# Attention scores: two 64-row matmuls on two halves of the array in place of two 128-row ones

## The chip, the cores and the metric

The kernel runs on one core of a Trainium2 chip. The metric is device microseconds from the start to the end of one execution; three runs of the kernel before were timed, and one execution was profiled with all its instructions.

The engines are named as in the profile: PE is TensorE's matmul, PEld its weight load, DVE is VectorE, ACT ScalarE, POOL GpSimd, SP the engine whose queue issues the DMAs. A matmul in this program is always two instructions: a weight load of the stationary operand (LDWEIGHTS, on PEld) and the product with the moving operand (MATMUL, on PE). The array has 128 rows, over which a product contracts, and 128 columns.

## What is computed

The reference is one layer of a hybrid backbone: a gated linear attention and a differential attention run on the same normalised input, are gated, merged and projected. The change lies in the differential attention alone:

```
def diff_attention(q1, q2, k1, k2, v, lam):
    ...
        s1 = jnp.einsum('bhqd,bhkd->bhqk', qb1, k1).astype(jnp.float32) * scale
        s2 = jnp.einsum('bhqd,bhkd->bhqk', qb2, k2).astype(jnp.float32) * scale
        a = jax.nn.softmax(s1, axis=-1) - lam * jax.nn.softmax(s2, axis=-1)
        return jnp.einsum('bhqk,bhkv->bhqv', a.astype(v.dtype), v)
```

There are 8 heads, 1024 latent queries, and 1280 keys (256 of the context, then 1024 latent ones). Each head has two components, with queries and keys of their own (q1, k1 and q2, k2, 64 numbers each) and one value matrix of 128 columns. Everything is float32.

## The kernel before

**High and low parts.** PE multiplies numbers rounded to a shorter form (fp32r) in one pass. The kernel keeps accuracy by splitting a float32 operand into a rounded part, "high", and the rest, "low", and by adding up several products. For the scores the four products high by high, high by low, low by high and low by low fit into two matmuls, because a component has only 64 numbers and the array has 128 rows. A key tile holds the high parts of a component's keys in rows 0 to 63 and the low parts in rows 64 to 127, over all 1280 keys. A query tile holds the high queries (`Q[comp][:, 0]`) and the low queries (`Q[comp][:, 1]`), each written twice, in rows 0 to 63 and again in rows 64 to 127. The matmul with index j = 0 therefore gives high queries by (high + low keys), the one with j = 1 low queries by (high + low keys), and PSUM adds them up.

**A unit of the scores.** `att_scores` (line 1940) runs over 8 heads and 8 query tiles of 128 queries: 64 units. A unit's scores take five PSUM banks of 512 columns: two for the main part of component 0 (keys 0 to 1023), one shared by the tails of both components (keys 1024 to 1279 of component 0, keys 0 to 255 of component 1), and two for the main part of component 1 (keys 256 to 1279). In the tables at lines 2035 and 2036 each pair is the first key and the number of keys:

```
    TAIL = ((1024, 256), (0, 256))
    MAIN = (((0, 512), (512, 512)), ((256, 512), (768, 512)))
```

The helper `score` (line 1952) issues the two matmuls, j = 0 and j = 1, of one stretch of keys. So the main part of a component is four matmuls with 512 moving columns: bank 0 with j = 0 and 1, then bank 1 with j = 0 and 1. The tails add four matmuls with 256 columns. After the main part, VectorE takes the maximum over both banks (`att_max`, line 1991), and ScalarE makes the exponentials with their sum (`att_exp`, line 1998); VectorE joins the two components (`att_mix`), PE transposes the result (`att_tr`), its parts are split into high and low, and PE multiplies them with the values (`att_av`).

**What sets the order.** The program is written out once, by a planner (class `Driver`, line 59). Tasks are generators; a task that is due issues its instructions, and the planner keeps a clock of PE (`now`) and of the other engines with a cost for each instruction, so that each engine's instructions stand in an order fixed before the run. `mm` (line 348) issues a matmul and charges PE, for fp32r, 0.009 us plus 0.000428 us for each moving column, 0.228 us for 512 columns. A `yield AtPE(0)` lets other due tasks go in between. The order of the parts of the attention (scores "S", transposes "T", values "A") is a list made by `att_order` (line 1915). Gaps in PE's plan are filled with other projections' matmuls (`fill`, line 2194; in the profile "mb<-h,wt").

`banked` (line 359) tells the framework which PSUM bank an instruction of the scores touches, so that only instructions of other engines on the same bank are waited for.

**Loading keys and queries.** `att_keys` (line 1848) loads a head's keys: for each component one DMA of 64 rows by 1280 high parts and one of the low parts, from scratch in DRAM into one of three key buffers (the tile "hk" in the profile). The buffers are given back after the head's last query tile. `att_queries` (line 1873) loads the queries of two query tiles at a time, each part twice. All these DMAs are issued from SP's queue.

Of the kernel before, what the change touches and what calls it, by code (L numbers as in the profile page):

```python
# [20 lines left out]
P = 128  # L21
# [3 lines left out]
T = S + CTX  # L25
# [207 lines left out]
class Hybrid:  # L233
# [20 lines left out]
        mm=("psA", 3), tp=("psA", 2), edge=("sbE", 1), gs=("psA1", 1), go=("psA1", 1), gt=("psA1", 1),  # L254
# [90 lines left out]
            yield  # L345
        self.d.spawn(later(), AtPE(at), prio=-9)

    def mm(self, out, lhsT, rhs, start, stop, more=False):
        self.ins = self.nc.tensor.matmul(out, lhsT, rhs, start=start, stop=stop, skip_group_check=more).ins  # L349
        n = rhs.free_size()  # L350
        c = 0.009 + max(n, 230) * 0.000428 if rhs.dtype == F32R else 0.006 + max(4 * n, 470) / 2400
        return self.d.op("PE", c, [out], [lhsT, rhs])

    def mm3(self, out, sh, sl, mh, ml, first, last, more=False):
        self.mm(out, sh, mh, first, False, more)
# [1492 lines left out]
    def att_keys(self):  # L1848

        for hd in range(8):  # L1850
            c, x = hd // 4, hd % 4
            for i in range(10):
                yield self.ev_st["dk", c, i]
            if hd:
                yield self.ev_q[0, 1]
            else:
                yield self.gla_free[3]
                yield from self.acq("hc", 16)
                Driver.places = (T, 2 * T, 3 * T)
                self.hk = self.t("hk", [P, HK], F32R)  # L1860
            K = []
            for comp in range(2):
                rows = slice(64 * comp, 64 * comp + 64)
                yield from self.acq("kk")
                m = (2 * hd + comp) % 3
                kt = self.hk[:, m * T:(m + 1) * T]
                self.dma(kt[0:64], self.d_kT[0][c][x, rows])
                self.dma(kt[64:128], self.d_kT[1][c][x, rows])
                K.append(kt)
            self.K[hd] = K  # L1870
            self.d.set(self.ev_k[hd], self.d.when(*K))
# [68 lines left out]
    def att_scores(self):  # L1940

        nc, d = self.nc, self.d
        yield self.ev_b
        s5 = self.t("s5", [P, 2 * T])
        for hd in range(8):
            for qt in range(8):
                pr, qs = qt // 2, slice((qt % 2) * P, (qt % 2) * P + P)
                yield self.ev_k[hd]
                yield self.ev_q[hd, pr]
                K, Q = self.K[hd], self.Q[hd, pr]  # L1950

                def score(po, comp, o, n):
                    bank = po.offset % (2 * T) // 512
                    for j in range(2):
                        e = self.mm(po, Q[comp][:, j, qs], K[comp][:, o:o + n], j == 0, j == 1)
                        self.banked(self.ins, "PE", bank)
                    return e

                u = dict(hd=hd, qt=qt, E=[None, None], mt=self.t("sm", [P, 2]), mx=[self.t("sm", [P, 1]) for _ in range(2)],
                         z=self.t("sm", [P, 2]), left=2, ev=[Event() for _ in range(3)])  # L1960

                for comp in range(2):
                    yield from self.acq(f"s{comp}")
                    pm = s5[:, 1536 * comp:1536 * comp + 1024]
                    if comp == 0:
                        yield from self.turn("S", 8 * hd + qt, 0)
                    if self.flush:
                        self.flush(1)
                    for x, (o, n) in enumerate(self.MAIN[comp]):
                        e = score(pm[:, x * 512:(x + 1) * 512], comp, o, n)  # L1970
                        if x == 0:
                            yield AtPE(0)
                    self.passed("S", 8 * hd + qt, comp)
                    d.spawn(self.att_max(u["ev"][comp], u["mx"][comp], pm, 3 * comp, 3 * comp + 1), On(e, "DVE"), prio=-3)
                    yield AtPE(0)
                    if comp == 0:
                        yield from self.acq("st")
                        yield from self.turn("S", 8 * hd + qt, 1)
                        pt = s5[:, 1024:1536].rearrange("p (c k) -> p c k", c=2)
                        for x in range(2):  # L1980
                            e = score(pt[:, x], x, *self.TAIL[x])
                        d.spawn(self.att_max(u["ev"][2], u["mt"], pt, 2), On(e, "DVE"), prio=-3)
                    elif qt == 7:
                        self.rel("kk", e, 2)
                    d.spawn(self.att_exp(u, comp, s5), On(e, "DVE"), prio=-3)
                    yield AtPE(0)
                if qt % 2 == 1:
                    self.rel(*(("aq", e, 2) if hd or pr else ("raw", e)))
                d.set(self.ev_u[8 * hd + qt])
# [42 lines left out]
        d.set(self.ev_a[u["hd"], u["qt"]], e)  # L2032


    TAIL = ((1024, 256), (0, 256))
    MAIN = (((0, 512), (512, 512)), ((256, 512), (768, 512)))
    GROUPS = ((0, 4), (4, 4), (8, 2))
# [773 lines left out]
```

## Time and profile before

| | |
|---|---|
| runs of the kernel before | 1616.01, 1616.22, 1618.52 us; median 1616.22 |
| span of the profiled execution, first to last instruction | 1614.1 us |
| median of the runs less that span | 2.1 us |
| granted TensorE clock, mean over the span | 1.000 |
| scores on PE, first and last start | 898.8 and 1422.8 us |
| weight loads of the scores, median | 188 ns |
| maxima on DVE (`sm<-s`), 192 of them | 193.3 us busy |
| exponentials on ACT (`e<-s,sm`), 128 of them | 169.3 us busy |
| key loads (`hk<-d_kT`), 32 of 320 KB | 5.9 us from issue to landing, median |

The span is the time from the first to the last instruction of the one profiled execution; a run's time also holds what lies around it. "Busy" is the time in which an engine has an instruction in work; a matmul's recorded duration contains the way through the array, so that consecutive matmuls overlap in the record, and the distance between their starts tells how long each holds the array. A form such as `128*128 128x512` is the stationary operand's rows by columns, then the moving operand's rows by columns. The profile prints fp32r operands of PE as f32. All matmuls are issued from line 349 and all transposes from line 375, so groups are told apart by their tiles: "s" scores, "b<-at,vv" values, "b<-ident,e" transposes, "mb<-h,wt" fill.

### The profile page before, as it was taken

The page shows a single profiled execution, that of the slowest core. Times are in us where ns is not written, and L with a number is a line of the kernel's source. Part 1 is how long each engine was busy: PE and PEld are TensorE (multiplying, and loading weights), DVE is VectorE, ACT ScalarE, POOL GpSimd, SP SyncE. Part 2 cuts the span into 40 slices and gives each one's busy share as a digit, 9 for nine tenths or more (in the row PEclk, how much of TensorE's full clock was granted, in tenths as well). Part 3 has the DMA queues.
Part 4 walks back from the last instruction along what each step waited for, and adds up shares of the span by engine and source line. Part 5 has one row for each costly group of instructions (what it writes and reads, how often), then busy time and mean ns, then how long its engine had stood idle before and what let it go on. Part 6 is the DMA issues. An engine that isn't in the chain of part 4 may idle for free.

```text
span 1614.1 us, 24349 instructions
## 1 busy us (share of the span) xinstructions
PE 1591.4 (99%) x8229; PEld 1328.1 (82%) x8229; DVE 1224.4 (76%) x2118; ACT 835.7 (52%) x1720; POOL 634.3 (39%) x663
## 2 busy tenths in 40 slices
PE   8999999999999999999999999999999999999999
PEld 3788888888888888888888788888888888888887
DVE  4787945676777779767677688878778888888994
ACT  4776523435343454555535566665665666656331
POOL 1500000001415667535564256656765666560000
PEclk9999999999999999999999999999999999999999
DMA  8576996998878367564645944545587545347662
GB/s 305 201 257 239 329 304 232 344 331 295 278 238 281 116 194 235 167 212 118 189 118 158 253 121 121 151 129 151 150 264 218 159 137 150 111 155 285 204 206 100
DMA packets 259565, 331.16 MB, mean 205 GB/s; under 512 B 22600, under 2 KB 160752, under 8 KB 259440
## 3 DMA queue, kind: packets, MB, share of 16 engines
q1 hardware_dynamic: 259440, 329.60, 63.8%
q8 instruction: 65, 1.06, 0.3%
q14 instruction: 60, 0.49, 0.1%
HBM read 225.20 MB, written 104.33 MB: 204 GB/s over the span
## 4 chain that ended last, share of the span: by engine, by line
PE 89%; DVE 4%; issue 2%; DMA 2%; ACT 1%; POOL 1%; SPq 0%; ACTq 0%; DVEq 0%; POOLq 0%
PE mm L349 30%; PE mb L349 11%; PE s L349 8%; PE mc L349 7%; PE b L349 6%; PE tp L349 5%; PE gt L349 5%; PE b L375 5%; PE go L349 4%; PE gs L349 4%; PE mz L349 2%; PE tp L375 2%; DVE sm L201 1%; POOL at L201 1%; DMA w<-in_w_ada 1%
## 5 line engine op out<-in xcount | busy, mean ns | idle before, releaser
L349 PE MATMUL mm<-w,h 128*128 128x512 f32 x912 | 231.0, 400 | 0.0
L349 PE MATMUL mb<-h,wt 128*128 128x512 f32 x840 | 223.0, 400 | 0.0
L201 DVE TENSOR_REDUCE sm<-s 128x1 f32<-128x1024 f32 (+1 forms) x192 | 193.3, 1037 | 10.7 <-PE s L349 6.6
L201 ACT ACTIVATE e<-s,sm 128x1280 f32<-128x1280 f32 x128 | 169.3, 1329 | 54.4 <-DVE sm L201 51.2
L349 PEld LDWEIGHTS mm<-w,h 128*128 128x128 f32 x912 | 167.4, 188 | 32.8
L201 POOL TENSOR_TENSOR at<-ac,at 128x512 fp32r<-128x512 f32 x128 | 188.2, 1471 | 10.7
L349 PEld LDWEIGHTS mb<-h,wt 128*128 128x128 f32 x840 | 151.4, 188 | 28.6 <-DVE ft L201 0.3
L201 POOL TENSOR_SCALAR at<-ac 128x512 fp32r<-128x512 f32 x128 | 96.9, 757 | 191.0 <-ACT ac L201 190.7
L349 PE MATMUL s<-hk,aq 128*128 128x512 f32 x744 | 169.0, 363 | 1.9 <-ACT e L201 1.8
L349 PE MATMUL mm<-h,w 128*128 128x512 f32 x672 | 168.2, 400 | 1.0 <-DVE h L201 1.0
L349 PEld LDWEIGHTS mm<-h,w 128*128 128x128 f32 x672 | 123.7, 188 | 26.4 <-DVE h L201 1.5
L201 DVE TENSOR_TENSOR w<-raw,w 128x512 fp32r<-128x512 f32 x128 | 96.0, 766 | 54.2 <-ACT w L201 52.0
L349 PEld LDWEIGHTS s<-hk,aq 128*128 128x128 f32 x744 | 117.7, 189 | 18.5 <-ACT e L201 3.6
L349 PE MATMUL b<-at,vv 128*128 128x256 f32 x960 | 130.1, 287 | 1.1 <-ACT ac L201 0.8
L349 PEld LDWEIGHTS b<-at,vv 128*128 128x128 f32 x960 | 119.5, 191 | 2.8 <-ACT ac L201 1.0
L201 ACT ACTIVATE w<-raw 128x512 fp32r<-128x512 f32 x128 | 78.1, 626 | 84.2 <-PE tp L349 23.8
L201 ACT ACTIVATE ac<-b 128x512 f32<-128x512 f32 x122 | 72.5, 598 | 91.8 <-PE b L375 91.7
L201 POOL TENSOR_TENSOR sm<-sm,nhalf 128x2 f32<-128x2 f32 (+2 forms) x94 | 107.7, 1146 | 27.9 <-DVE sm L201 22.7
L201 DVE SCALAR_TENSOR_TENSOR e<-e,sm,e 128x1280 f32<-128x1280 f32 x64 | 117.9, 1842 | 1.0
L349 PE MATMUL mm<-w,g 128*128 128x512 f32 x432 | 105.7, 389 | 0.0
L349 PEld LDWEIGHTS mm<-w,g 128*128 128x128 f32 x432 | 81.1, 188 | 16.9
L375 PE MATMUL b<-ident,e 128*128 128x128 f32 x610 | 92.6, 273 | 1.3 <-ACT ac L201 0.8
(357 smaller groups left out, 3054.2 us busy)
## 6 DMA issues: line engine op xcount, KB each, us to landing
raw<-in_w_in SPq DMA_DIRECT2D x62, 512.0 KB, 4.3
g<-d_s SPq DMA_DIRECT2D x32, 640.0 KB, 6.2
g<-d_s SPq DMA_DIRECT2D x32, 512.0 KB, 5.7
aq<-d_qT SPq DMA_DIRECT2D x124, 128.0 KB, 3.4
d_dv<-pl SPq DMA_DIRECT2D x40, 256.0 KB, 3.9
gv<-d_v SPq DMA_DIRECT2D x40, 256.0 KB, 3.3
d_kT<-pl SPq DMA_DIRECT2D x40, 256.0 KB, 2.8
hk<-d_kT SPq DMA_DIRECT2D x32, 320.0 KB, 5.9
```

What stands on the lines that cost most here:

```text
L201: self.ins = f(out, *args, **kw).ins
L349: self.ins = self.nc.tensor.matmul(out, lhsT, rhs, start=start, stop=stop, skip_group_check=more).ins
L375: self.nc.tensor.transpose(out, src, self.ident[:n, :n])
```

## The change

```
-    def mm(self, out, lhsT, rhs, start, stop, more=False):
+    def mm(self, out, lhsT, rhs, start, stop, more=False, cost=1.0):
         self.ins = self.nc.tensor.matmul(out, lhsT, rhs, start=start, stop=stop, skip_group_check=more).ins
         n = rhs.free_size()
         c = 0.009 + max(n, 230) * 0.000428 if rhs.dtype == F32R else 0.006 + max(4 * n, 470) / 2400
-        return self.d.op("PE", c, [out], [lhsT, rhs])
+        return self.d.op("PE", c * cost, [out], [lhsT, rhs])
...
                 kt = self.hk[:, m * T:(m + 1) * T]
-                self.dma(kt[0:64], self.d_kT[0][c][x, rows])
-                self.dma(kt[64:128], self.d_kT[1][c][x, rows])
+                for j in range(2):
+                    for h, cs in ((j, slice(0, self.SWAP[comp])), (1 - j, slice(self.SWAP[comp], T))):
+                        self.dma(kt[64 * h:64 * h + 64, cs], self.d_kT[j][c][x, rows, cs])
                 K.append(kt)
...
-                def score(po, comp, o, n):
-                    bank = po.offset % (2 * T) // 512
-                    for j in range(2):
-                        e = self.mm(po, Q[comp][:, j, qs], K[comp][:, o:o + n], j == 0, j == 1)
-                        self.banked(self.ins, "PE", bank)
+                def score(po, comp, o, n, j, rows=slice(0, P), cost=1.0):
+                    e = self.mm(po, Q[comp][rows, j, qs], K[comp][rows, o:o + n], j == 0, j == 1, cost=cost)
+                    self.banked(self.ins, "PE", po.offset % (2 * T) // 512)
                     return e
...
                     for x, (o, n) in enumerate(self.MAIN[comp]):
-                        e = score(pm[:, x * 512:(x + 1) * 512], comp, o, n)
+                        score(pm[:, x * 512:(x + 1) * 512], comp, o, n, 0)
                         if x == 0:
                             yield AtPE(0)
+                    for x, (o, n) in enumerate(self.MAIN[comp]):
+                        e = score(pm[:, x * 512:(x + 1) * 512], comp, o, n, 1, slice(64 * x, 64 * x + 64), float(x))
...
                         for x in range(2):
-                            e = score(pt[:, x], x, *self.TAIL[x])
+                            for j in range(2):
+                                e = score(pt[:, x], x, *self.TAIL[x], j)
...
+    SWAP = (512, 768)
     TAIL = ((1024, 256), (0, 256))
     MAIN = (((0, 512), (512, 512)), ((256, 512), (768, 512)))
```

The main part of a component is still four matmuls with 512 moving columns, in another order: high queries by bank 0's keys, high queries by bank 1's keys, low queries by bank 0's keys, low queries by bank 1's keys. The last two contract over 64 rows only. The one of bank 0 uses rows 0 to 63 of queries and keys, the one of bank 1 rows 64 to 127. So that both meet high keys there, a key tile now has its parts the other way round from the second bank on (from key 512 for component 0, key 768 for component 1: `SWAP`): low parts in rows 0 to 63, high parts in rows 64 to 127. That makes four DMAs of a component's keys in place of two, with the same bytes. The product of low queries and low keys is no longer in the main part. A matmul over all 128 rows, as all of j = 0 and the tails are, gives the same sum whichever half holds the high parts, since the queries stand in both halves.

The planner is told that the first of the two 64-row matmuls costs nothing and the second one whole matmul.

## The prediction

> **What bounds the kernel now.** I read the page first (shares of the engines, the chain that ended last), then the stretches of the attention stage, then who waited for whom there.
>
> ```profile
> span 1614.1 us, 24349 instructions
> PE 1591.4 (99%) x8229; PEld 1328.1 (82%) x8229; DVE 1224.4 (76%) x2118; ACT 835.7 (52%) x1720; POOL 634.3 (39%) x663
> ...
> PE 89%; DVE 4%; issue 2%; DMA 2%; ACT 1%; POOL 1%; SPq 0%; ACTq 0%; DVEq 0%; POOLq 0%
> ```
>
> PE is busy in 99% of the span and makes 89% of the chain. The view of the tile "s", the scores, gives their number, their durations (least, median, most, in ns) and their times:
>
> ```profile
> L349 PE MATMUL s<-hk,aq x744: 274/389/499, 911.0 to 1422.8; 128*128 128x512 f32 x124, 128*128 128x256 f32 x62
> L349 PE MATMUL s<-hk,raw x24: 274/389/499, 898.8 to 909.3; 128*128 128x512 f32 x16, 128*128 128x256 f32 x8
> ```
>
> 744 + 24 = 768 matmuls, 64 units (8 heads by 8 query tiles) of 12: two components with four products over 512 columns each, and four over 256 columns for the tail. A stretch of this stage, with the busy us of PE, PEld, DVE, ACT and POOL, the granted clock, DMA share and GB/s:
>
> ```profile
> 1100.00:1200.00 100.00, 99.32 (x617) 87.18 (x617) 82.29 (x155) 61.72 (x129) 63.19 (x58) 1.00 0.62 182
> ```
>
> PE is full, the clock whole, and DVE next with 82.29 of 100 us. The waits of PE between 900 and 1425 us (total us, times, longest) are all of these:
>
> ```profile
> PE s L349 <- ACT e L201: 2.0, 3, 1.3
> PE b L375 <- DVE b1k L201: 1.1, 3, 0.4
> PE b L375 <- ACT ac L201: 0.8, 1, 0.8
> PE b L349 <- ACT ac L201: 0.8, 1, 0.8
> PE b L375 <- DVE at L201: 0.3, 1, 0.3
> ```
>
> Together 5.0 us. So time taken from PE's queue in this stage, or put into it, should reach the end almost whole.
>
> How long a matmul occupies PE is not its recorded duration (389 ns, with the pipeline's depth in it) but the distance from one to the next, which the chain in order of time shows:
>
> ```profile
> 1102.59 2.15 PE b L349 x18
> ...
> 1106.61 0.93 PE s L349 x4
> 1107.54 1.37 PE mb L349 x6
> ```
>
> Four 512-column scores take 0.93 us, 0.23 each; six 512-column products of the fill 1.37, 0.228 each; eighteen of 256 columns 2.15, 0.119 each. The difference of 0.109 us for 256 columns is 0.43 ns a column, 0.218 for 512.
>
> **The change, part by part.** 128 times (64 units by two components), the two matmuls with the low queries change. They contract over 128 rows now, one after the other; afterwards they contract over 64, one over rows 0 to 63 into one bank, the other over rows 64 to 127 into the next. No instruction goes: 512 matmuls with 512 columns stay 512, each with its weight load. The product low by low, which the second one held, is dropped.
>
> *What it may remove.* If the array runs the two side by side, the second hides behind the first: 0.23 us for each pair, 128 x 0.23 = 29.4 us.
>
> *What it adds.* Every pair stands between full-height matmuls: before it the two products of the high queries, after it the tail, fill or transposes. So 256 times the array goes from 128 rows to 64 or back. Nearly all matmuls of the old kernel have full height, but a few small transposes have not, and twice one of these is followed at once by a full one (the two bursts below, then a place without such a change and the usual length of a transpose, all but the last from the view in order of time):
>
> ```profile
> 24.58 0.20 PE L375 MATMUL gt<-ident,p 2*128 2x2 f32 x1
> 24.70 0.33 PE L375 MATMUL tp<-ident,g 128*128 128x128 f32 x1
> ...
> 24.70 0.20 PEld L375 LDWEIGHTS tp<-ident,g 128*128 128x128 f32 x2
> ...
> 45.97 0.20 PE L375 MATMUL gt<-ident,p 4*128 4x4 f32 x1
> 46.10 0.33 PE L375 MATMUL tp<-ident,g 128*128 128x128 f32 x1
> ...
> 46.09 0.20 PEld L375 LDWEIGHTS tp<-ident,g 128*128 128x128 f32 x2
> ...
> 1106.92 0.62 PE L349 MATMUL s<-hk,aq 128*128 128x512 f32 x2
> ...
> 1107.15 0.19 PEld L349 LDWEIGHTS mb<-h,wt 128*128 128x128 f32 x1
> ...
> L375 PE MATMUL b<-ident,e 128*128 128x128 f32 x610 | 92.6, 273 | 1.3 <-ACT ac L201 0.8
> ```
>
> In the rows in order of time the first number is the start, the second the length. Without a change of height (the rows at 1106.92) the second score begins 0.23 later, at 1107.15, and the next weight load begins there too: it is hidden beneath the running matmul. Where a 2-row or 4-row transpose is followed by a full one, the full one's weight load begins 0.12 us after the small one started (24.58 to 24.70, 45.97 to 46.09), though the small one streams only 2 or 4 columns, and the row names no releaser. The full matmul then lasts 0.33 where such a transpose has 0.273, so it really began 0.06 later. From small to full is thus 0.19 us where nothing but 0.002 of streaming is to be done: the array is held for 0.12, and the weights are loaded afterwards, exposed.
>
> The Trainium skill, "TensorEngine Tiling (Array Packing)", section "Key Properties", says that changing the tiling mode drains TensorE, while going from tile to tile in one mode does not. The 0.12 us agrees with it; by that rule each pair pays two drains, and the sum is the one below, not the 29.4 us.
>
> For an fp32r score the exposed load is longer than the transpose's 0.06: the row of scores has a median of 389 and a longest of 499 ns, and the longest is a matmul that starts after idle time: 0.110 us of load. Hence:
> - Into the pair: 0.218 of streaming, 0.12 held, 0.110 load = 0.448 instead of 0.23, so +0.218.
> - Out of the pair: the same +0.218 where a score or the fill follows, and 0.218 + 0.19 - 0.23 = +0.178 where a transpose does; I take 0.20.
> - The second tile's own weight load: at best beneath the first's (0), at worst behind it (0.110). In the small mode loads follow closer, four within 0.32 us with the last taking 0.14, so 0.06 apart; I take 0.06.
>
> ```profile
> 45.76 0.32 PEld L375 LDWEIGHTS gt<-ident,p 4*128 4x128 f32 x4 [0.76 <-DVE p L201]
> ...
> 45.94 0.14 PEld L375 LDWEIGHTS gt<-ident,p 4*128 4x128 f32 x1
> ```
>
> Sum for one pair: 0.218 + 0.20 + 0.06 - 0.23 = +0.248 us, for 128 pairs +31.7 us. The upper bound is 0.218 + 0.218 + 0.110 - 0.23 = +0.316, or +40 us. The lower one has the loads run beneath the hold: 2 x (0.218 + 0.12 - 0.23) - 0.23 = -0.014, or -2 us. I take the sum, since both bursts show the load after the hold. The cover for none of it is there: PE is full.
>
> *What comes back.* With PE later and all others as before, the 5.0 us of PE's waits should vanish: -5.0.
>
> *Order.* Within a component, the high product of the second bank now comes before the low product of the first, and other work can slip in after one matmul instead of two. The last of the four still releases VectorE's maximum, so nobody waits for another event. The planner charges 0 for the first tile and one matmul for the second: 128 x 0.228 = 29 us less PE time in its plan, so later work is lined up against a PE clock that runs ahead. It shifts fill between stretches and no amount of it; I charge 0, bounded by the 5.0 us of waits either way.
>
> *Transfers.* Keys come in four DMAs for a component in place of two, the same bytes:
>
> ```profile
> L314 SPq DMA_DIRECT2D hk<-d_kT x32: 460/588/1730, 887.2 to 1356.3; - x32
> ...
> DMA to landing us min/median/max: 3.9/5.9/8.5
> ```
>
> 32 more issues at 0.588 us are 18.8 us of SP's queue over 470 us, 2.4 us for each head. Query loads for the next pair and the fill's weights stand behind them on SP. No DMA is among PE's waits in this stage, and the fill covers the change of head; I charge 0. Without that cover it would be 2 issues for the component that comes last, 1.2 us for each head, under 10 us in all.
>
> Sum: +31.7 - 5.0 = +26.7 us. The span would go from 1614.1 to 1640.8. The median of the runs, 1616.22, stands 2.1 above the span, which I keep: 1642.9.
>
> **The rivals.**
>
> *No hold for 64-row tiles: faster.* Tiles of 64 rows may follow full ones without a hold; the traces show only 2- and 4-row tiles, in one direction, with no matmul of 512 columns before. Then all 29.4 us are won, less some 0.01 a pair: about 1588. The DVE would stand at 82.29 of 95 us, still free. It decides from the point where the two steps together cost less than 0.23 us, 0.115 each; against it are two bursts which both show 0.12 with the load still to come. The Trainium skill, "TensorE: Matmul & The Clock Gate", section "Measured speedup vs the span model", counts about 4 ns for each further tile of a packed group and nothing for entering it; by that the time is this rival's, and no run here shows it yet.
>
> *No hold, but the second tile's load only begins with the first tile's matmul.* Then 0.23 - 0.110 = 0.12 us a pair is won, 15 us: 1601. For it: in this trace a load begins when the matmul before it starts, never earlier.
>
> *Holds and no side-by-side run.* The two tiles go one after the other: 256 steps at about 0.21 less 5.0 are +49: about 1665. Against it: the tiles share neither rows nor banks.
>
> *It does nothing or cancels.* Either no hold and no side-by-side run, or the hold with loads hidden (-2): 1616.
>
> **How the numbers follow.** Forecast (holds, loads exposed, tiles side by side) 0.58; its own range, with the bounds above and half of the waits, is 1625 to 1657. Faster whole 0.20, faster in part 0.09, no change 0.07, holds without side by side 0.06. A change under 0.2% (3.2 us) is what this kernel's runs can't tell from none. Faster 0.20 + 0.09 = 0.29, same 0.07, slower 0.58 + 0.06 = 0.64. For 8 in 10 the range must reach to the first rival: 1587 to 1657 leaves out the last but one case and the tails.
>
> **What would show it.** In the groups by shape, 256 score matmuls with 64 rows in place of 128. In order of time, the two of a pair starting within 0.1 us of each other (side by side) or 0.23 apart (not). Before the first and after the second, PEld idle by 0.1 to 0.3 us instead of 0.04. PE's waits for ACT and DVE smaller. It is wrong if the weight load after the pair starts while the pair still runs: then the rival without a hold is right. It would be wrong in its cover if PE waits for hk's DMA at a change of head.

## The result and the profile after

The changed kernel takes 1637.05 us (median; 1636.5 to 1637.55), the kernel before, on the same chip, 1617.37 (1616.01 to 1619.8). The ratio is 1.012, with a 95% interval of 1.0105 to 1.0134: slower by 19.4 us. The forecast was 1642.9, 26.7 us above the 1616.22 that it started from, in a range of 1587 to 1657.

The page of the changed kernel, span and busy time of the engines:

```profile
span 1634.6 us, 24414 instructions
...
PE 1611.8 (99%) x8229; PEld 1296.3 (79%) x8229; DVE 1217.7 (74%) x2118; ACT 834.0 (51%) x1720; POOL 648.0 (40%) x663
```

As many matmuls as before, PE just as full, and a span that is 20.5 us longer. So the time is PE's own. The tile "s" shows that the scores now end at 1442.6 instead of 1422.8 us:

```profile
L349 PE MATMUL s<-hk,aq x744: 274/397/504, 911.7 to 1442.6; 128*128 128x512 f32 x124, 128*128 128x256 f32 x62
```

The shapes at the end of the line are a sample, every fourth matmul, which happens to miss the 64-row ones. Nearly all of the loss thus arises inside the score stage. The weight loads of the scores grouped by shape, first before, then after; behind the bar stand busy us and mean ns, then the idle us of PEld just before them and what ended it:

```profile
L349 PEld LDWEIGHTS s<-hk,aq 128*128 128x128 f32 x744 | 117.7, 189 | 18.5 <-ACT e L201 3.6
```

```profile
L349 PEld LDWEIGHTS mb<-h,wt 128*128 128x128 f32 x840 | 146.7, 188 | 45.8 <-issue 16.6 <-ACT b1k L201 1.7 <-DVE ft L201 1.7
L349 PEld LDWEIGHTS s<-hk,aq 128*128 128x128 f32 x496 | 70.3, 190 | 8.3 <-ACT e L201 3.5 <-ACT at L201 1.7 <-ACT ac L201 0.5
L349 PEld LDWEIGHTS s<-hk,aq 64*128 64x128 f32 x248 | 23.1, 183 | 44.0 <-issue 44.0
```

The 248 loads with 64 rows of this group (124 pairs; the other four read the tile "raw") have 44.0 us of idle time before them, all put down to "issue", that is to nothing that the profile can name. That is 0.355 us for each pair. The loads of 128 rows in the same stage have 8.3 us over 496. The fill's loads, 77 of which follow a pair, have 16.6 us of the same unnamed sort. One pair in order of time, first PEld, then PE:

```profile
1109.27 0.19 PEld L349 LDWEIGHTS s<-hk,aq 64*128 64x128 f32 x2 [0.37 <-issue]
...
1109.70 0.19 PEld L349 LDWEIGHTS s<-hk,aq 128*128 128x128 f32 x1 [0.24 <-ACT at L201]
...
1108.95 0.40 PE L349 MATMUL s<-hk,aq 128*128 128x512 f32 x1
...
1109.27 0.50 PE L349 MATMUL s<-hk,aq 64*128 64x512 f32 x2
...
1109.71 0.39 PE L349 MATMUL s<-hk,aq 128*128 128x256 f32 x1
```

The last 128-row score starts at 1108.95. It streams for 0.218 us. The loads of the pair do not begin beneath it, but 0.32 after its start: the array is held for 0.10. Then both loads go together (two in 0.19, where one takes 0.183), and both matmuls too: two within 0.50 us, their starts 3 to 4 ns apart in all 128 pairs. Each is recorded with 0.50 instead of 0.39, since it starts 0.11 late, behind its exposed load. The next load of 128 rows comes 0.43 after them, and its matmul is again 0.11 late. Its row names ACT as the end of the idle time, but 0.43 is also the distance behind pairs where it names "issue", and the mean over the pairs.

From the start of a component's second 128-row product to the true start of what follows the pair (a matmul's recorded end less the usual length of its form), the mean is 0.846 us over the 123 pairs that stand beside no wait; for the same 123 in full_rows below, with the same order and 128 rows, it is 0.689. A pair thus costs 0.157 us, and 128 of them 20.1.

### The profile page after: what moved, and what is told of

Read it like the earlier page. It is cut to its first block, busy times and chain, and to the rows that moved or that the text cites. A ratio compares the mean times of both kernels' runs of the same rounds, so it can differ in the third digit from the quotient of the medians.

```text
span 1634.6 us, 24414 instructions
## 1 busy us (share of the span) xinstructions
PE 1611.8 (99%) x8229; PEld 1296.3 (79%) x8229; DVE 1217.7 (74%) x2118; ACT 834.0 (51%) x1720; POOL 648.0 (40%) x663
## 5 line engine op out<-in xcount | busy, mean ns | idle before, releaser
L349 PE MATMUL mb<-h,wt 128*128 128x512 f32 x840 | 232.6, 410 | 0.8 <-DVE ft L201 0.3
L201 DVE TENSOR_REDUCE sm<-s 128x1 f32<-128x1024 f32 (+1 forms) x192 | 194.4, 1037 | 21.8 <-PE s L349 19.4
L201 POOL TENSOR_TENSOR at<-ac,at 128x512 fp32r<-128x512 f32 x128 | 197.5, 1543 | 10.7
L349 PEld LDWEIGHTS mb<-h,wt 128*128 128x128 f32 x840 | 146.7, 188 | 45.8 <-issue 16.6
L201 POOL TENSOR_SCALAR at<-ac 128x512 fp32r<-128x512 f32 x128 | 105.6, 825 | 183.5 <-ACT ac L201 181.7
L349 PEld LDWEIGHTS s<-hk,aq 128*128 128x128 f32 x744 | 93.4, 187 | 52.3 <-issue 44.5
L201 DVE SCALAR_TENSOR_TENSOR e<-e,sm,e 128x1280 f32<-128x1280 f32 x64 | 114.4, 1788 | 0.9
```

What stands on the lines that cost most here:

```text
L201: self.ins = f(out, *args, **kw).ins
```

## The experiments

Theory 1 says that each change of height holds the array and exposes a load, 256 times, and that the pair does run side by side. Theory 2 says that the new order, the key DMAs or the planner's clock make the loss. Theory 3 says that 64-row matmuls are slower by themselves. Ratios are to the kernel before on the same chip, with 95% intervals; differences are worked out from the ratios, times 1618 us.

**Full rows.**

```
-  e = score(pm[:, x * 512:(x + 1) * 512], comp, o, n, 1, slice(64 * x, 64 * x + 64), float(x))
+  e = score(pm[:, x * 512:(x + 1) * 512], comp, o, n, 1, slice(0, P), float(x))
```

> The changed kernel with one thing undone: the two low-query matmuls contract over all 128 rows again. Their new place in the order, the four key DMAs with swapped parts and the planner's costs stay. Theory 1 (each change between 128 and 64 rows holds the array, 256 times): all of the loss goes, 1617 within 3 us. Theory 2 (order, transfers or the planner's clock cost the time): nearly all of it stays, about 1637. Theory 3 (a 64-row matmul is itself slower): 1617 too.

1621.26 us, ratio 1.0017 (1.0008 to 1.0026): 2.8 us above the kernel before. Its instructions on PE, DVE, ACT and POOL stand in exactly the order of the changed kernel. So of the 19.4 us, 16.7 hang on the 64 rows and nothing else (1.012 less 1.0017), and 2.8 on the rest of the change. Its scores end at 1427.0, those of the changed kernel at 1442.6:

```profile
L349 PE MATMUL s<-hk,aq x744: 274/390/499, 912.1 to 1427.0; 128*128 128x512 f32 x124, 128*128 128x256 f32 x62
```

**Both tiles on one half.** Keys are loaded in four DMAs, not swapped.

```
-  for h, cs in ((j, slice(0, self.SWAP[comp])), (1 - j, slice(self.SWAP[comp], T))):
+  for h, cs in ((j, slice(0, self.SWAP[comp])), (j, slice(self.SWAP[comp], T))):
...
-  e = score(..., comp, o, n, 1, slice(64 * x, 64 * x + 64), float(x))
+  e = score(..., comp, o, n, 1, slice(0, 64), float(x))
```

> Both 64-row matmuls of a pair on rows 0 to 63, with keys in four DMAs but not swapped, so that they share their rows and cannot run side by side; the changes of height stay 256. If the pair does run side by side in the changed kernel, one matmul of 0.23 us comes back 128 times: 1637 + 29 = 1666. If it gains nothing there: 1637. Theory 2: 1637.

1666.79 us, ratio 1.0295 (1.028 to 1.0309), 28.3 us above the changed kernel, with the instructions in the same order. One pair of it in order of time, PEld and PE:

```profile
1114.24 0.29 PEld L349 LDWEIGHTS s<-hk,aq 64*128 64x128 f32 x2 [0.37 <-issue]
1114.90 0.20 PEld L375 LDWEIGHTS b<-ident,b1k 128*128 128x128 f32 x2 [0.37 <-issue]
...
1114.24 0.50 PE L349 MATMUL s<-hk,aq 64*128 64x512 f32 x1
...
1114.58 0.39 PE L349 MATMUL s<-hk,aq 64*128 64x512 f32 x1
```

On the same rows the second matmul starts 0.34 after the first, 0.11 of it the first one's load, and so 0.23 behind it; its own load is hidden (0.39, not 0.50). The two loads take 0.29 together here, the second starting 0.108 after the first in all pairs, where on two halves they take 0.19. The changed kernel does win what it set out to win, one matmul for each pair, 28 us. Against full_rows the 256 changes of height cost 0.0278 x 1618 = 45.0 us, 0.176 each.

**Tiles set apart.** Each 64-row matmul follows its own bank's 128-row one:

```
   for x, (o, n) in enumerate(self.MAIN[comp]):
       score(pm[:, x * 512:(x + 1) * 512], comp, o, n, 0)
+      e = score(pm[:, x * 512:(x + 1) * 512], comp, o, n, 1, slice(64 * x, 64 * x + 64), float(x))
       if x == 0:
           yield AtPE(0)
-  for x, (o, n) in enumerate(self.MAIN[comp]):
-      e = score(pm[:, x * 512:(x + 1) * 512], comp, o, n, 1, slice(64 * x, 64 * x + 64), float(x))
```

> The two 64-row matmuls are set apart: each follows the 128-row one of its own bank, so there are 512 changes of height instead of 256, and nothing runs side by side. Theory 1, with 0.20 us for each change from the changed kernel's trace: 1617 + 512 x 0.20 = 1719, from 1710 to 1725. Theory 2: about 1637. Theory 3, where the excess hangs on the 256 matmuls of 64 rows and not on the changes: 0.2 us each, 1617 + 51 = 1668.

1713.14 us, ratio 1.0587 (1.0572 to 1.0601). Against full_rows 0.057 x 1618 = 92.2 us for 512 changes of height: 0.180 each. Twice the changes cost twice the time, while the number of 64-row matmuls stayed at 256. Theory 3 (1668) falls. The page has the same sign, twice as large as in the changed kernel's page (44.5 there):

```profile
L349 PEld LDWEIGHTS s<-hk,aq 128*128 128x128 f32 x744 | 122.3, 187 | 97.1 <-issue 91.2
```

**The planner told the truth.**

```
-  ... slice(64 * x, 64 * x + 64), float(x))
+  ... slice(64 * x, 64 * x + 64), 1.4)
```

> The changed kernel, with the planner told what a pair really occupies: 1.4 matmuls for each of the two, 0.64 us together, instead of 0 and 1. Theory 1: 1637 within 3 us, as the planner's clock only sets the order of work that PE has to do anyway. Theory 2, if the planner's clock is the cause: 1617 to 1625.

1655.71 us, ratio 1.0228 (1.0214 to 1.0242): 17.5 us slower than the changed kernel, which neither theory expected. The groups of the score stage, first of the changed kernel, then of this one:

```profile
L349 PE MATMUL mb<-h,wt 128*128 128x512 f32 x795 | 221.4, 411 | 0.8 <-DVE ft L201 0.3
```

```profile
L349 PE MATMUL s<-hk,aq 128*128 128x512 f32 x744 | 170.7, 402 | 8.1 <-ACT e L201 7.4
L349 PE MATMUL mb<-h,wt 128*128 128x512 f32 x585 | 166.0, 413 | 0.5 <-ACT ft L201 0.3 <-DVE ft L201 0.2
...
L375 PE MATMUL b<-ident,e 128*128 128x128 f32 x604 | 95.1, 278 | 11.1 <-DVE b1k L201 4.8 <-DVE at L201 4.0 <-ACT ac L201 2.3
```

With pairs charged 0.64 us the plan put 585 matmuls of the fill beside the scores instead of 795, and PE waited for ACT and DVE: the listed waits of the stage are 20.9 us instead of 3.8. The price of the tiles had not changed: from the second high product to the pair it is 0.427 us in both. The cover had.

**The charge alone, without tiles, and with them.**

```
-  ... slice(0, P), float(x))          # full_rows
+  ... slice(0, P), 1.0)               # full_rows_cost
...
-  ... slice(64 * x, 64 * x + 64), float(x))     # the changed kernel
+  ... slice(64 * x, 64 * x + 64), 1.0)          # tiles_cost
```

> The run full_rows (all 128 rows for the low queries, in their new place in the order, four key DMAs) with the planner charged one whole matmul for each of the two, as in the kernel before. It splits the 3 us by which full_rows lay above the kernel before. If the plan's clock that runs ahead made them: 1618, as before. If the new order or the key DMAs made them: 1621.

> The changed kernel with the planner charged one matmul for each tile. Its PE, DVE, ACT and POOL instructions stand in exactly the order of full_rows_cost, as those of the changed kernel stand in the order of full_rows; the two pairs differ only in the rows of the low-query matmuls. In the first pair the tiles cost 1637.05 - 1621.26 = 15.8 us. If that is the chip's price for the changes of height, whatever the plan, this run is at 1624.4 + 15.8 = 1640, from 1636 to 1645. If it depends on the order as much as the nudged kernels do (4 to 9 us), anything from 1631 to 1650.

full_rows_cost: 1624.41 us, ratio 1.0035 (1.0022 to 1.0049). tiles_cost, with the same order of instructions: 1638.6, ratio 1.0123 (1.0106 to 1.014). The difference is 0.0088 x 1618 = 14.2 us. With 16.7 from the first pair of kernels of equal order, the tiles' price on the chip is 14 to 17 us under two plans, two differences whose intervals overlap. A part of the gap shows in the traces: transposes follow 67 pairs in tiles_cost and 32 in the changed kernel, and a transpose's exposed load is 0.056 us where that of the fill or a score is 0.11. full_rows_cost itself, at 1624.41, lies above both of its expected values (1618 and 1621); the two runs after it look for the reason.

**Keys alone, order alone, and two controls.** keys_only is the kernel before with the four swapped key DMAs of the diff. order_only is full_rows_cost with the two key DMAs of before. The controls change only the planner's charge for a score matmul of the kernel before:

```
-  e = self.mm(po, Q[comp][:, j, qs], K[comp][:, o:o + n], j == 0, j == 1)
+  e = self.mm(po, Q[comp][:, j, qs], K[comp][:, o:o + n], j == 0, j == 1, cost=1.02)   # nudge_down: 0.98
```

> The kernel before with one part of the change alone: a component's keys in four DMAs with swapped parts. All score matmuls have 128 rows and stand as before. The runs full_rows_cost and full_rows lay 6 and 3 us above the kernel before with no 64-row matmul. If the key DMAs cost that: 1622 to 1625. If they are covered: 1618 within 2.

> The kernel before with another part alone: the high product of the second bank ahead of the low product of the first; 128 rows everywhere, two key DMAs, one matmul charged for each. If the order makes the 6 us of full_rows_cost: 1622 to 1625. If it is free: 1618 within 2.

> A control: the kernel before, with nothing changed but the planner's charge for a score matmul, 2% more. The same instructions stand in a slightly other order. If an order that falls otherwise is worth several us by itself, as true_cost (+19) and by_unit_true (-8 against by_unit) suggest, it moves by 2 to 6 us in either direction; if the planner's charge matters only when far off, 1618 within 2.

> The same control with 2% less for a score matmul: 2 to 6 us in either direction if small differences of order count by themselves, 1618 within 2 if not.

| kernel | median us | ratio (95%) |
|---|---|---|
| keys_only | 1618.58 | 1.0001 (0.9992 to 1.001) |
| order_only | 1625.57 | 1.0047 (1.0033 to 1.0061) |
| nudge_up | 1627.11 | 1.0059 (1.0045 to 1.0073) |
| nudge_down | 1622.53 | 1.0028 (1.0018 to 1.0038) |

The key DMAs are covered. The new order costs 7.6 us, but a planner's charge that is 2% off, up or down, costs 9.5 (more than the 2 to 6 that I had expected) and 4.5 without any change to the work. So the part of the loss that is not the tiles need not be a price of "high before low": it lies within what another plan of the same work makes.

**One group for each unit.** The low products of both components stand together after the second component's high ones, so that a unit has two changes of height instead of four; `LOWC` is 1.0 in by_unit and 1.9 in by_unit_true.

```
+  for comp in range(2):
+      for x, (o, n) in enumerate(self.MAIN[comp]):
+          e = score(main(comp, x), comp, o, n, 1, slice(64 * x, 64 * x + 64), self.LOWC[comp] * x)
+      d.spawn(self.att_max(...), On(e, "DVE"), prio=-3)
+      d.spawn(self.att_exp(u, comp, s5), On(e, "DVE"), prio=-3)
```

> The 64-row matmuls of both components of a unit in one group of four, so that there are 128 changes of height instead of 256 while all pairs run side by side. The planner is charged 0 and 1 matmul for a pair, as in the change. Holds and exposed loads of 0.18 us a change (from full_rows to one_half and to apart): full_rows 1621 + 128 x 0.18 - 128 x 0.23 = 1615, from 1611 to 1621. If a change between tiles of the same height held the array too, or the second pair's loads were exposed, 0.1 to 0.2 us more for each of 64 units: 1622 to 1628. Rival: the maximum of component 0 now starts later, PE waits for ACT and DVE, and it ends above 1625.

> The run by_unit, with the planner charged what a pair with its share of the changes occupies, 1.9 matmuls. The run true_cost was 19 us slower than the changed kernel because the plan then put 585 instead of 795 fill matmuls beside the scores and PE waited 22 us instead of 5. If the plan's clock matters in that way here too, this one is slower than by_unit by 5 to 15 us, as its charge is off by less; if not, it is equal within 3 us.

by_unit: 1678.55 us, ratio 1.0372 (1.0358 to 1.0386); by_unit_true: 1670.04, ratio 1.0321 (1.0307 to 1.0335). I had expected 1615, and the sign of the charge the other way round. The array did what theory 1 says. One group of by_unit in order of time, PEld and PE:

```profile
1110.62 0.30 PEld L349 LDWEIGHTS s<-hk,aq 64*128 64x128 f32 x4 [0.37 <-issue]
1111.28 0.30 PEld L349 LDWEIGHTS mb<-h,wt 128*128 128x128 f32 x2 [0.36 <-issue]
...
1110.62 0.50 PE L349 MATMUL s<-hk,aq 64*128 64x512 f32 x2
...
1110.96 0.40 PE L349 MATMUL s<-hk,aq 64*128 64x512 f32 x2
```

The second pair starts 0.34 after the first, 0.11 of it load, and is not held: it lasts 0.40, with no load of its own to see. But the stretches of by_unit, with PE, PEld, DVE, ACT, POOL, clock, DMA share and GB/s, and the groups between 1400 and 1480 us show what happened to the kernel:

```profile
1300.00:1400.00 100.00, 98.30 (x589) 79.67 (x587) 75.12 (x143) 53.90 (x113) 53.97 (x50) 1.00 0.50 150
1400.00:1500.00 100.00, 81.47 (x447) 60.90 (x446) 73.81 (x140) 54.35 (x113) 59.96 (x53) 0.81 0.24 71
```

```profile
L349 PE MATMUL s<-hk,aq 64*128 64x512 f32 (+2 forms) x110 | 33.0, 506 | 5.4 <-ACT e L201 5.1
L375 PE MATMUL b<-ident,e 128*128 128x128 f32 x91 | 17.3, 308 | 7.5 <-ACT ac L201 7.2 <-DVE at L201 0.3
...
L349 PE MATMUL mb<-h,wt 128*128 128x512 f32 x15 | 4.0, 404 | 0.0
```

The scores last until 1479.4 us, and in their last 80 us only 15 fill matmuls are left; in the kernel before there are 119 in its last 80 (1340 to 1420):

```profile
L349 PE MATMUL mb<-h,wt 128*128 128x512 f32 x119 | 32.1, 400 | 0.0
```

PE then waits for the chain through the maximum and the exponentials, which start later for component 0, and its granted clock falls to 0.81. The rival named in the expectation decided, but it left out the clock: the mean granted clock of by_unit is 0.983 over a span of 1678.1 us, by my estimate up to 28.5 us lost, beside listed waits of 31.9 us between 890 and 1500. How the two share the loss was not separated. Whether a plan fitted to the group would win is open: by the array alone it would be 0.197 + 0.191 - 2 x 0.23 = -0.07 us a unit, some 4.6 us won in all, as much as a nudge.

## Why the prediction was right, step by step

*The range.* It was wide: from 1587 it took in two cases in which the change wins, so that a time inside it says little. The test is the forecast's own case, 1625 to 1657, and 1637.05 lies in it, 5.9 us below the forecast.

*The bound.* Right in the main: PE stayed full, and 16 of the 20.1 us put into PE's queue in the stage reached the end of the trace.

*The hold.* Right in kind and nearly in size, though read from 2- and 4-row transposes: 0.10 us, into the pair and out of it, against 0.12. The rival without a hold falls, with the one in which a load begins only with the matmul before it. The sign against it, a load that starts while the pair still runs, is not met: the pair above is recorded until 1109.77, but its last column has entered by 1109.60 (1109.27 + 0.11 + 0.218), and the load starts at 1109.70.

*Into and out of the pair.* Forecast +0.218 and +0.20. From the true starts of the same 123 pairs: into it 0.319 to the load and 0.108 of load, less 0.23, is +0.197; out of it +0.205 where a matmul of fp32r follows and +0.151 where a transpose does (32 times), +0.191 in the mean.

*The second tile's load.* This is the term that was mis-sized: forecast 0.06, measured 0.003 to 0.004 from load to load. It is over 7 of the 11.6 us by which the sum of +31.7 exceeded the trace's 20.1; the two steps make the rest. The 0.06 was read from four small loads that all go to the same rows, and the tiles of a pair have rows of their own: on the same rows, in one_half, the second load does come 0.108 later.

*Side by side.* Right: 0.23 us a pair, 28.3 us from one_half.

*What comes back.* Forecast 5.0 us by PE's waits, all of them. About 4 came back, and the waits did not all go: 3.8 us are left in the changed kernel, of 5.7 in full_rows. The spans of these two are 16.1 us apart, against 20.1. Matmul by matmul, the distances within all 128 pairs grew by 18.9 us in sum, since waits beside five pairs took up 1.2; all other distances of the stage shrank by 2.6. The 0.1 left over lies outside the stage.

*Transfers.* Right: 0, from keys_only.

*Order.* Charged at 0 with a bound of 5.0 us, the sum of PE's waits in the old plan. That bound was wrong. It took the waits of one plan for all that a plan can be worth; the controls moved by 4.5 and 9.5 us, true_cost by 17.5. In the changed kernel it came to 2.8, and this hid a part of the excess of the second load: that the forecast came within 5.9 us owes something to luck.

## What to carry to other kernels

Two 64-row matmuls on two halves of the array do save one matmul, but only while the array stays at that height: here each change between 128 and 64 rows took 0.18 us, so a pair of 512 columns (0.23 saved) does not pay for two changes. By the array's times two such pairs in a row just would (0.39 against 0.46), but the two runs that tried it lost more in their plans, so no run here shows it. The price of a change of this sort can be found in an old trace, in any place where a small operand is followed at once by a full one, by the distance from one load to the next; here that gave the hold to 0.02 us. In a kernel whose order is planned by a cost model, compare variants with the same order of instructions, and nudge the plan once as a control, before a few us are put down to an edit.

## What was not expected of the hardware

Two weight loads on different halves of the array ran together: both within 0.19 us, one alone 0.183, two on the same half 0.29. Between two pairs of the same height there was no hold (0.34 from start to start, 0.11 of it the first pair's load). The time lost in a change from 128 to 64 rows is not named by any wait: the profile books all 44.0 us of PEld's idle time before the pairs as "issue".
